# The first stage of a pool, retention and expert layer, cut into two phases without GpSimd's arithmetic, with the pool's window means moved among the gate products

## The chip, the cores and the metric

The kernel runs on one core of one Trainium2 chip. The metric is the device time of one execution in microseconds. TensorE does the matrix products, VectorE (DVE) and ScalarE (ACT) prepare their operands, GpSimd (POOL) helps with elementwise work and issues some transfers, and SyncE (SP) issues the loads of the weights.

## The reference, cut to what matters

512 tokens, width 2048, everything in fp32. What the change touches is the first half of the layer:

```python
mod = silu(c) @ w_ada + b_ada                       # 6 parts of 2048: sh1, sc1, g1, sh2, sc2, g2
hn = rmsnorm(x, norm_mix_gain) * (1 + sc1) + sh1
u_pool, q, k, v, g_ret, a_pool, a_ret = split(hn @ w_in)
pooled[g] = causal_window_mean(u_pool[g], w) - u_pool[g]     # g = 0..3, w = 2, 4, 8, 16
pool_out = (pooled[g] @ pool_w[g]) * pool_scale
q, k = rotary(q), rotary(k) / 16
y = retention(q, k, v)                              # 8 heads
merged = sigmoid(a_pool) * (pool_out @ w_branch_pool) + sigmoid(a_ret) * ((silu(g_ret) * layernorm(y)) @ w_branch_ret)
x = x + g1 * (merged @ w_out)
```

Then come the experts' queries, a selection among 16384 experts and two large products with their tables; the change does not touch them.

## The kernel before, in words

The activations stand transposed, as 16 tiles of 128 channels by 512 tokens. Each fp32 product is three matrix products of rounded operands (`mm3`, L85 to L87): a weight or activation is split into a high half (`whc`, `act`; ACT's cast at L73) and a low half (`wlc`, `act`; a subtraction at L74). A product of one block of 128 outputs (`gemm_t`) is 16 contraction steps, 48 matrix products; it takes its weights as two half chunks, and `half` converts the next half chunk while one is used. Weights arrive in chunks of 1 MB (`rawc`), loaded by SP's queue in the order of the list in `main_chunks`. There are three buffers each for `whc` and `wlc`.

`start` is the first stage. Its product for the first eight blocks of `u_pool` runs over the contraction outside and the blocks inside, since each channel's scale is found only then: for contraction step k, a chunk of `w_ada` is multiplied by silu(c) and summed on DVE (L188), the bias is added (L335), the scale is formed (L281), the input tile is scaled and split (L347 on ACT, L356 on DVE), and 24 matrix products run. `low_engine` puts the low halves of the weights on POOL here. POOL also adds up the squares (L205), and DVE fills in the rotary tables (L419 to L454). A second product over eight blocks follows in `pool_branch`, with the window sums (`window`, L513 and around) and four small products with `pool_w` (`mix`) between its blocks; then `shift` adds the shift of the modulation to all 16 tiles: POOL adds the halves (L397), DVE multiplies with 1/rms (L398), ACT and DVE split again (L403, L404). The retention needs the shifted tiles: its first product is q of head 0. After the eight heads come 32 gate products (`branches`, L670), whose results go to DRAM (`sig`), and then the products with the branch weights.

Inside `manual_schedule` the instructions of an engine stand as the code is written; elsewhere a scheduler orders them. Each engine works through its own queue in order.

Of the kernel before, what the change touches and what calls it, by code (L numbers as in the profile page):

```python
# [9 lines left out]
FT = mybir.dt.float32  # L10
# [19 lines left out]
POOL_JOBS = [('up', 0), ('up', 1), ('mix', 0), ('up', 2), ('up', 3), ('mix', 1), ('up', 4), ('up', 5), ('mix', 2), ('up', 6), ('up', 7), ('mix', 3)]  # L30
POOL_ADA = [1, 1, 1, 1, 2, 2, 2, 2, 2, 2, 0, 0]
# [16 lines left out]
class Mixer:  # L48
# [235 lines left out]
    def start(self):  # L284
        nc, a = self.nc, self.a
        stt = nc.vector.scalar_tensor_tensor
        self.cond_scope = ExitStack()
        cp = self.cond_scope.enter_context(self.tc.tile_pool(name="cp", bufs=1))
        with ExitStack() as cs:
            tp = lambda n, b=1: cs.enter_context(self.tc.tile_pool(name=n, bufs=b))  # L290
            p1, tmp, ap = tp("st1"), tp("st2", 3), tp("st3", 3)
            with self.tc.manual_schedule():
# [9 lines left out]
                seq = [(*self.ada(KT), ap), (a["w_up0"][0], None)]  # L302
                for k in range(1, KT):
# [4 lines left out]
                self.stream(seq + self.main_chunks())  # L308
                load(1)
                self.total = cp.tile([P, T], FT, name="total")  # L310
                banks = [self.bank() for _ in range(8)]
                self.hn = []
                raws = []
                table = self.rotary_tables(tmp)
                next(table)

                def low_half():
                    t, i = raws.pop(0)
                    h = self.wh.tile([P, D // 2], FR, name="whc")
                    l = self.wl.tile([P, D // 2], FR, name="wlc")  # L320
                    self.split(t[:, i * 1024:(i + 1) * 1024], h, l, nc.gpsimd)
                    self.ready.append((h, l))
# [6 lines left out]
                squares = 0  # L329

                def scale_in():
                    k = len(scaled)
                    self.consume()
                    m = slice(KT + k, KT + k + 1)
                    nc.vector.tensor_tensor(out=self.mod[:, m], in0=self.mod[:, m], in1=self.bada[:, m], op=OP.add)  # L335
                    self.scale_of(1, 0, 0, k)
                    scaled.append(self.sc[:, 0, k:k + 1])
                scaled = []
                scale_in()
                weights()  # L340
                low_half()
                for k in range(KT):
                    if k == 12:
                        self.ahead = 3
# [3 lines left out]
                    if k == 0:  # L348
                        stt(out=l, in0=xk[k], scalar=scaled[k], in1=h.bitcast(FT), op0=OP.mult, op1=OP.subtract)
                    if k + 1 < KT:  # L350
                        scale_in()
                        if k % 2:
                            weights()
                        low_half()
                    if k:
                        stt(out=l, in0=xk[k], scalar=scaled[k], in1=h.bitcast(FT), op0=OP.mult, op1=OP.subtract)  # L356
                    self.hn.append((h, l))
                    wh, wl = self.ready.pop(0)
# [5 lines left out]
                    if k >= 4:  # L364
                        for _ in (0, 1):
                            if squares < KT:
                                self.square(self.total, xk[squares], squares == 0, tmp, nc.gpsimd)
                                squares += 1
                    if k >= 2:
                        next(table, None)  # L370
                        next(table, None)
                for _ in table:
                    pass
                self.warm_sqrt(self.ones[:, 0:1])
                self.low_engine = nc.gpsimd
                self.convert()
                for i in (0, 1):
                    u = self.ring.tile([P, T], FT, name="act")
                    nc.scalar.copy(out=u, in_=banks[i])
                    banks[i] = u  # L380
                dg = self.diagonals(self.token_rms([self.total], cp), cp)
                self.r = cp.tile([P, T], FT, name="r")
                self.after(1, lambda: nc.scalar.copy(out=self.r, in_=self.spread(dg)))
                banks.append(self.gemm_t(self.hn))
            self.first_banks = banks

    def shift(self, pool):

        nc = self.nc
        m = slice(0, KT)
        nc.vector.tensor_tensor(out=self.mod[:, m], in0=self.mod[:, m], in1=self.bada[:, m], op=OP.add)
        for k, (h, l) in enumerate(self.hn):
            z = pool.tile([P, T], FT, name="hn")
            nc.gpsimd.tensor_tensor(out=z, in0=h.bitcast(FT), in1=l.bitcast(FT), op=OP.add)  # L397
            nc.vector.tensor_tensor(out=z, in0=z, in1=self.r, op=OP.mult)  # L398
            self.shifted(z, self.mod[:, k:k + 1], h, l)

    def shifted(self, z, sh, h, l):
        nc = self.nc
        nc.scalar.activation(out=h, in_=z, func=AF.Identity, bias=sh, scale=1.0)  # L403
        nc.vector.scalar_tensor_tensor(out=l, in0=z, scalar=sh, in1=h.bitcast(FT), op0=OP.add, op1=OP.subtract)  # L404

    def rotary_tables(self, tmp):
        nc, a = self.nc, self.a
        ts, stt = nc.vector.tensor_scalar, nc.vector.scalar_tensor_tensor
        self.cos = self.const.tile([P, T], FT, name="cos")
        self.sin = self.const.tile([P, T], FT, name="sin")  # L410
        invf = self.const.tile([P, 1], FT, name="invf")
        nc.gpsimd.dma_start(out=invf, in_=a["inv_freq"])
        pos = tmp.tile([P, T], I32, name="sq")
# [4 lines left out]
        r, h, n = self.sin, self.cos, tmp.tile([P, T], FT, name="rot", bufs=1)  # L418
# [37 lines left out]
    def main_chunks(self):  # L456
        a = self.a
        first = []
        for i, (what, n) in enumerate(POOL_JOBS):
            first.append((a["w_up1"][n] if what == "up" else a["pool_w"][GROUPS[n]], None))  # L460
            first += [self.ada(k) for k in range(sum(POOL_ADA[:i]), sum(POOL_ADA[:i + 1]))]
# [5 lines left out]
        seq += [a["w_ap"][i] for i in range(KT)] + [a["w_ar"][i] for i in range(KT)]  # L467
# [16 lines left out]
    def pool_branch(self):  # L484
# [3 lines left out]
        with ExitStack() as cs:  # L488
            tp = lambda n, b: cs.enter_context(self.tc.tile_pool(name=n, bufs=b))
            up, pk, ob, cp = tp("pu", 6), tp("pk", 8), tp("po", 3), tp("pc", 1)  # L490
            cnt = cp.tile([P, 4, PAD], FT, name="cnt")
            nc.gpsimd.dma_start(out=cnt, in_=a["inv_count"].to_broadcast([P, 4, PAD]))
            pooled = [[] for _ in GROUPS]

            def evacuate(bank):
                u = up.tile([P, PAD + T], FT, name="u")
                nc.vector.memset(u[:, :PAD], 0.0)
                nc.scalar.copy(out=u[:, PAD:], in_=bank)
                return u

            def window(turn, bank, raw=None):
                g = GROUPS[turn]
                u = evacuate(bank) if raw is None else up.tile([P, PAD + T], FT, name="u")
                if raw is not None:
                    nc.vector.memset(u[:, :PAD], 0.0)
                nc.vector.tensor_tensor(out=u[:, PAD:], in0=u[:, PAD:] if raw is None else raw, in1=self.r, op=OP.mult)
                s = u
                for lvl in range(g + 1):
                    w = 1 << lvl
                    s2 = up.tile([P, PAD + T], FT, name="u")  # L510
                    if lvl < g:
                        nc.vector.memset(s2[:, :PAD], 0.0)
                    nc.vector.tensor_tensor(out=s2[:, PAD:], in0=s[:, PAD:], in1=s[:, PAD - w:PAD + T - w], op=OP.add)  # L513
                    s = s2
                q = ob.tile([P, T], FT, name="pq")
                w = 2 << g
                nc.vector.tensor_tensor(out=q[:, :w], in0=s[:, PAD:PAD + w], in1=cnt[:, g, :w], op=OP.mult)
                nc.vector.tensor_tensor(out=q[:, :w], in0=q[:, :w], in1=u[:, PAD:PAD + w], op=OP.subtract)
                nc.vector.scalar_tensor_tensor(out=q[:, w:], in0=s[:, PAD + w:], scalar=1.0 / w, in1=u[:, PAD + w:],
                                               op0=OP.mult, op1=OP.subtract)  # L520
                h = pk.tile([P, T], FR, name="ph")
                l = pk.tile([P, T], FR, name="pl")
                self.split(q, h, l)
                pooled[turn].append((h, l))
# [19 lines left out]
            for what, i in POOL_JOBS:  # L544
                if what == "up":
                    window(2 + i // 4, self.gemm_t(self.hn) if i else self.first_banks[8])
                else:
                    if i == 3:
                        self.shift(ob)
# [766 lines left out]
```

## Time and profile before

| | |
|---|---|
| median of 3 runs | 4974.7 us (4973.16 to 4975.7) |
| profiled execution, its own time | 4985.34 us |
| its span | 4983.6 us |
| TensorE busy | 97% of the span |
| DVE, ACT, POOL busy | 65%, 34%, 32% |
| mean granted TensorE clock | 0.988 |

The profiled execution is 10.6 us longer than the median of the runs. A busy TensorE in these views includes the time in which matrix products overlap, so an idle TensorE is what to look for. The granted clock is given as a share of 2.4 GHz; it has two levels, 1.2 and 2.4 GHz.

### The profile page before, as it was taken

How to read it: one execution, taken by the hardware profiler on the slowest of the kernel's cores; microseconds unless marked ns; L12 is line 12 of the kernel's file. 1: busy time of each engine (PE TensorE's matmuls, PEld its weight loads, DVE VectorE, ACT ScalarE, POOL GpSimd, SP SyncE). 2: the span in 40 equal slices, each digit the busy share in tenths (PEclk: the TensorE clock that was granted, in tenths of full speed). 3: DMA queues.
4: the chain of work that ended last, by engine and by line, in shares of the span. 5: the costliest groups of instructions: out<-in, count | busy, mean ns of one | idle time of the engine just before them, and what ended most of it. 6: DMA issues, size and time to landing. Idle time of an engine off the chain costs nothing.

```text
span 4983.6 us, 58696 instructions
## 1 busy us (share of the span) xinstructions
PE 4832.4 (97%) x22905; PEld 4173.4 (84%) x22905; DVE 3237.4 (65%) x4296; ACT 1704.9 (34%) x2703; POOL 1570.5 (32%) x1125
## 2 busy tenths in 40 slices
PE   6889999999999999999989999999999999999998
PEld 5668888888888888888878999999999888888887
DVE  8873334434332245655567998888787688888876
ACT  3332222222222222222232346556566433332233
POOL 6440000000000010000010367777788344444433
PEclk9999999999999999999999999999999999999999
DMA  6442222222233356765732577887888989898884
GB/s 265 178 148 87 102 102 99 95 102 95 92 126 131 125 190 227 263 228 204 237 107 99 172 275 282 291 295 275 308 294 314 327 310 326 317 332 323 316 284 152
DMA packets 268454, 1058.12 MB, mean 212 GB/s; under 512 B 22656, under 2 KB 73904, under 8 KB 173328
## 3 DMA queue, kind: packets, MB, share of 16 engines
q1 hardware_dynamic: 208960, 726.71, 42.2%
q0 software_dynamic: 54416, 325.48, 17.2%
q8 instruction: 181, 2.97, 0.2%
q10 hardware_dynamic: 4800, 2.16, 0.2%
q14 instruction: 97, 0.79, 0.0%
HBM read 973.53 MB, written 80.75 MB: 212 GB/s over the span
## 4 chain that ended last, share of the span: by engine, by line
PE 72%; DVE 11%; issue 8%; DMA 5%; POOL 2%; ACT 2%; SPq 0%; POOLq 0%; DVEq 0%; ACTq 0%
PE bank L87 24%; PE bank L85 24%; PE bank L86 24%; DVE wlc L74 2%; DVE urow L978 1%; DVE rawc L188 1%; DMA gd<-gsc 1%; DMA rawc<-in_w_ada_dram 1%; POOL ohx L918 1%; DVE u L513 1%; DMA x<-m 1%; ACT whc L73 1%; PE bank L907 1%; DVE gsc L898 0%; DVE eq L869 0%
## 5 line engine op out<-in xcount | busy, mean ns | idle before, releaser
L74 DVE TENSOR_TENSOR wlc<-rawc,whc 128x1024 fp32r<-128x1024 f32 x905 | 1158.3, 1286 | 993.5 <-ACT whc L73 992.9
L73 ACT CAST whc<-rawc 128x1024 fp32r<-128x1024 f32 x968 | 998.9, 1050 | 1995.4 <-PE bank L86 1093.8
L85 PE MATMUL bank<-act,whc 128*128 128x512 f32 x2816 | 1101.8, 391 | 27.8 <-ACT act L347 19.0
L86 PE MATMUL bank<-act,whc 128*128 128x512 f32 x2816 | 1102.8, 392 | 24.1 <-DVE act L356 20.2
L87 PE MATMUL bank<-act,wlc 128*128 128x512 f32 x2816 | 1102.1, 391 | 6.4 <-POOL wlc L74 3.6
L87 PE MATMUL bank<-fh,wlc 128*128 128x384 f32 (+1 forms) x2304 | 792.7, 344 | 15.6 <-DVE wlc L74 12.9
L85 PE MATMUL bank<-fh,whc 128*128 128x384 f32 (+1 forms) x2304 | 793.3, 344 | 4.8 <-ACT whc L73 2.8
L86 PE MATMUL bank<-fl,whc 128*128 128x384 f32 (+1 forms) x2304 | 791.1, 343 | 0.7 <-DVE fl L734 0.5
L86 PEld LDWEIGHTS bank<-act,whc 128*128 128x128 f32 x2816 | 531.8, 189 | 141.0 <-DVE act L356 24.8
L85 PEld LDWEIGHTS bank<-act,whc 128*128 128x128 f32 x2816 | 532.1, 189 | 138.8 <-ACT act L347 19.0
L87 PEld LDWEIGHTS bank<-act,wlc 128*128 128x128 f32 x2816 | 531.8, 189 | 120.3 <-POOL wlc L74 4.9
L918 POOL TENSOR_SCALAR ohx<-iota,tr,gh 128x128 fp32r<-128x128 f32 x384 | 586.9, 1535 | 75.1 <-PE bank L907 70.7
L85 PE MATMUL bank<-whc,ph 128*128 128x512 f32 x1536 | 602.7, 392 | 1.0 <-ACT ph L73 1.0
L87 PE MATMUL bank<-whc,pl 128*128 128x512 f32 x1536 | 600.5, 391 | 0.0
L86 PE MATMUL bank<-wlc,ph 128*128 128x512 f32 x1536 | 597.7, 389 | 1.6 <-DVE wlc L74 1.6
L87 PEld LDWEIGHTS bank<-fh,wlc 128*128 128x128 f32 x2304 | 436.0, 189 | 30.3 <-DVE wlc L74 16.1
L85 PEld LDWEIGHTS bank<-fh,whc 128*128 128x128 f32 x2304 | 436.5, 189 | 15.7 <-ACT whc L73 4.0
L86 PEld LDWEIGHTS bank<-fl,whc 128*128 128x128 f32 x2304 | 436.0, 189 | 11.3 <-DVE fl L734 2.0
L929 POOL DMA_INDIRECT vrow<-in_v_dram,eidx x128 | 273.7, 2138 | 488.4 <-DVE accg L1076 473.2
L188 DVE SCALAR_TENSOR_TENSOR rawc<-rawc,cond 128x2048 f32<-128x2048 f32 x96 | 241.8, 2520 | 198.7 <-DMA rawc<-in_w_ada_dram 198.7
L86 PEld LDWEIGHTS bank<-wlc,ph 128*128 128x128 f32 x1536 | 288.4, 188 | 65.0 <-DVE wlc L74 2.4
L87 PEld LDWEIGHTS bank<-whc,pl 128*128 128x128 f32 x1536 | 288.2, 188 | 64.8 <-DVE pl L74 0.3
(285 smaller groups left out, 5292.9 us busy)
## 6 DMA issues: line engine op xcount, KB each, us to landing
rawc<-in_ut_dram SPq DMA_DIRECT2D x128, 1024.0 KB, 5.7
rawc<-in_v_dram SPq DMA_DIRECT2D x128, 1024.0 KB, 7.5
rawc<-in_w_ada_dram SPq DMA_DIRECT2D x96, 1024.0 KB, 5.3
rawc<-in_w_v_dram SPq DMA_DIRECT2D x32, 1024.0 KB, 4.9
rawc<-in_w_g_dram SPq DMA_DIRECT2D x32, 1024.0 KB, 4.8
rawc<-in_w_br_dram SPq DMA_DIRECT2D x32, 1024.0 KB, 5.0
ga<-gao SPq DMA_DIRECT2D x64, 384.0 KB, 6.8
gd<-gsc SPq DMA_DIRECT2D x24, 1024.0 KB, 10.1
```

Source lines behind the costliest of these rows:

```text
L73: nc.scalar.copy(out=h, in_=src)
L74: (eng or nc.vector).tensor_tensor(out=l, in0=src, in1=h.bitcast(FT), op=OP.subtract)
L85: mm(out, w[0], x[0], start=start, stop=False)
L86: mm(out, w[0], x[1], start=False, stop=False)
L87: mm(out, w[1], x[0], start=False, stop=stop)
L188: nc.vector.scalar_tensor_tensor(out=t, in0=t, scalar=1.0, in1=self.cond, op0=OP.mult, op1=OP.mult, accum_out=self.mod[:, j:j + 1])
L513: nc.vector.tensor_tensor(out=s2[:, PAD:], in0=s[:, PAD:], in1=s[:, PAD - w:PAD + T - w], op=OP.add)
L907: nc.tensor.matmul(bank[:, u * 2 * P:(u + 1) * 2 * P], y, x.rearrange("p h i -> p (h i)"), start=True, stop=True)
L918: nc.gpsimd.tensor_scalar(out=x[:, 0, :], in0=self.iota, scalar1=tr[:, 0, s], scalar2=gh[:, s].bitcast(FT), op0=OP.is_equal, op1=OP.mult)
L929: self.nc.gpsimd.indirect_dma_start(out=t, out_offset=None, in_=src, in_offset=bass.IndirectOffsetOnAxis(ap=self.eidx[:, k:k + 1], axis=0))
L978: nc.vector.scalar_tensor_tensor(out=u, in0=u, scalar=1.0, in1=fnat, op0=OP.mult, op1=OP.mult, accum_out=act[:, i:i + 1])
```

## The change

`start` is written anew in two phases. In the first, the contraction-outside product for eight blocks, all low halves are made by DVE; the bias is folded into the forming of the scale (`one`, L334); the sums of squares and the tables are gone from it. In the second phase the other eight blocks follow as plain `gemm_t` products; between them DVE adds the squares and multiplies the inputs with 1/rms in place, and the block results go to DRAM (`u`, `rd`) by POOL's queue. Then `shift` makes the 16 shifted tiles from the inputs (ACT forms the tile, DVE rounds and subtracts), and the two products of q of head 0 run in `start`, contraction outside, as the shifted tiles come. The rotary tables are made at the start of `retention`. `pool_branch` now hands out `window` and `mix`, which `branches` calls between the 32 gate products; each window loads its sums from DRAM, and there DVE makes the low halves of `pool_w`.

```diff
-                    self.split(t[:, i * 1024:(i + 1) * 1024], h, l, nc.gpsimd)
...
+                def convert():
+                    t, i = raws.pop(0)
+                    pair = self.next_pair()
+                    self.split(t[:, i * 1024:(i + 1) * 1024], *pair)
+                    return pair
...
-                    nc.vector.tensor_tensor(out=self.mod[:, m], in0=self.mod[:, m], in1=self.bada[:, m], op=OP.add)
-                    self.scale_of(1, 0, 0, k)
...
+                    stt(out=o, in0=self.mod[:, KT + k:KT + k + 1], scalar=one[:, k:k + 1],
+                        in1=self.gains[:, 0, k:k + 1], op0=OP.add, op1=OP.mult)
...
+                self.after(7, lambda: found.append(self.token_rms([total], cp)))
+                self.after(8, lambda: found.append(self.diagonals(found[0], cp)))
+                self.after(9, spread)
+                for k in range(KT):
+                    self.after(10 + k // 3, lambda k=k: over_rms(k))
+                for n in range(8):
+                    b = self.gemm_t(self.hn)
+                    self.after(1, lambda b=b, n=n: evacuate(8 + n, b))
...
+                    nc.scalar.activation(out=z, in_=xk[k], func=AF.Identity, bias=self.mod[:, k:k + 1],
+                                         scale=self.sc[:, 0, k:k + 1])
+                    nc.vector.tensor_copy(out=h, in_=z)
+                    tt(out=l, in0=z, in1=h.bitcast(FT), op=OP.subtract)
...
+                for kk in range(8):
+                    step(0, 0, kk, a0)
+                    step(1, 0, kk, b0)
+                b1 = convert()
+                for kk in range(4):
+                    step(0, 1, kk, a1)
+                for kk in range(4):
+                    step(0, 1, 4 + kk, a1)
+                    step(1, 1, kk, b1)
...
-        self.low_engine = None
-        self.cond_scope.close()
...
+            for _ in self.rotary_tables(tmp):
+                pass
...
+            window, mix = self.pool_branch(cs)
+            work = [(t, i) for t in range(4) for i in range(4)]
+            for j in range(2 * KT):
+                if work and j % 6 < 4:
+                    window(*work.pop(0))
+                b = self.gemm_t(self.hn) if j else self.first_gate
...
+                if j in MIXES:
+                    mix(MIXES.index(j))
```

In DVE's queue, one contraction step of the first product stood like this (`rawc` is a chunk of `w_ada`, `act` the low half of a scaled input tile, `sin` and `cos` the tables):

```order
L188 SCALAR_TENSOR_TENSOR rawc,mod<-rawc,cond 128x2048
L335 TENSOR_TENSOR mod<-mod,bada 128x1
L281 SCALAR_TENSOR_TENSOR sc<-mod,gains 128x1
L356 SCALAR_TENSOR_TENSOR act<-x_108,sc,act 128x512
L423 TENSOR_SCALAR cos<-sin 128x512
L425 TENSOR_SCALAR cos<-cos 128x512
```

Now DVE's queue begins so, `wlc` being the low half of a half chunk of weights:

```order
L306 TENSOR_SCALAR one<-bada 128x16
L188 SCALAR_TENSOR_TENSOR rawc,mod<-rawc,cond 128x2048
L334 SCALAR_TENSOR_TENSOR sc<-mod,one,gains 128x1
L74 TENSOR_TENSOR wlc<-rawc,whc 128x1024
L342 SCALAR_TENSOR_TENSOR act<-x_110,sc,act 128x512
L188 SCALAR_TENSOR_TENSOR rawc,mod<-rawc,cond 128x2048
```

The low half of the weights has come to DVE, and the bias and the tables have left the step.

At the handover to the retention DVE's queue was this in the kernel before (the last windows, `pq`, `pl`, and the shifted tiles, `hn`, `act`, side by side):

```order
L404 SCALAR_TENSOR_TENSOR act<-hn,mod,act 128x512
L517 TENSOR_TENSOR pq<-u,cnt 128x2
L519 SCALAR_TENSOR_TENSOR pq<-u 128x510
L518 TENSOR_TENSOR pq<-pq,u 128x2
L404 SCALAR_TENSOR_TENSOR act<-hn,mod,act 128x512
L398 TENSOR_TENSOR hn<-hn,r 128x512
L74 TENSOR_TENSOR pl<-pq,ph 128x512
```

Now it is this, for the last three shifted tiles (`rp_1614` is a scratch tile of the tables; `act` of L406 and L407 are the two halves of a shifted tile):

```order
L406 CAST act<-rawc 128x512
L463 TENSOR_SCALAR cos<-cos 128x512
L407 TENSOR_TENSOR act<-rawc,act 128x512
L406 CAST act<-rawc 128x512
L465 SCALAR_TENSOR_TENSOR sin<-cos,sin 128x512
L407 TENSOR_TENSOR act<-rawc,act 128x512
L406 CAST act<-rawc 128x512
L467 SCALAR_TENSOR_TENSOR rp_1614<-cos,sin 128x512
L407 TENSOR_TENSOR act<-rawc,act 128x512
L74 TENSOR_TENSOR wlc<-rawc,whc 128x1024 x2
```

The windows are gone from there; six instructions of the tables, from L457 on, stand among the last six shifted tiles, and the low half of the last half chunk of q's weights stands behind all of them.

Among the gate products DVE's queue held nothing but 60 low halves in a row. Now a stretch between two of them reads so (`raw` is a block's sums, loaded from DRAM; `pq` the mean less the value):

```order
L74 TENSOR_TENSOR wlc<-rawc,whc 128x1024
L74 TENSOR_TENSOR pl<-pq,ph 128x512
L552 TENSOR_TENSOR u<-u 128x512
L544 MEMSET u 128x16
L545 TENSOR_TENSOR u<-raw,r 128x512
L556 TENSOR_TENSOR pq<-u,cnt 128x4
L558 SCALAR_TENSOR_TENSOR pq<-u 128x508
L557 TENSOR_TENSOR pq<-pq,u 128x4
L74 TENSOR_TENSOR wlc<-rawc,whc 128x1024
```

And POOL's queue, where the loads of `raw` stand between the stores of the gates, begins there with:

```order
L542 DMA raw<-u 128x512 x2
L674 DMA ret<-ro 128x512 x4
L533 DMA cnt<-in_inv_count_dram 128x64
L535 DMA r<-rd 128x512
L705 DMA sig<-sg 128x512
L542 DMA raw<-u 128x512 x3
L705 DMA sig<-sg 128x512
L542 DMA raw<-u 128x512 x2
```

The window work is spread between the low halves instead of standing ahead of one of them, and five loads are issued ahead of the second gate's store.

## Rows read from the trace of the kernel before

**Rows 1.** The page: TensorE's busy tenths in 40 slices of the span.

```profile
PE   6889999999999999999989999999999999999998
```

**Rows 2.** Stages: window, length; each engine's busy us (instructions); clock, DMA share, GB/s.

```profile
0.00:19.00 19.00, 0.03 (x1) 0.03 (x1) 2.83 (x6) 4.94 (x5) 4.71 (x13) 1.00 0.89 327
19.00:140.00 121.00, 99.26 (x384) 77.33 (x385) 108.68 (x100) 38.80 (x54) 85.81 (x36) 0.94 0.60 230
140.00:327.40 187.40, 147.93 (x593) 116.18 (x592) 172.70 (x228) 60.59 (x86) 97.83 (x50) 0.89 0.49 174
327.40:349.20 21.80, 21.80 (x97) 18.05 (x97) 11.19 (x12) 6.40 (x8) 4.05 (x6) 1.00 0.55 196
371.10:414.40 43.30, 43.30 (x193) 35.85 (x192) 15.81 (x18) 11.31 (x13) 0.00 (x0) 1.00 0.28 93
1480.00:1820.00 340.00, 340.00 (x1510) 281.76 (x1509) 85.29 (x76) 90.74 (x106) 24.89 (x47) 1.00 0.39 137
```

**Rows 3.** TensorE's waits from 19 to 330 us: total, times, longest.

```profile
PE bank L85 <- ACT ph L73: 23.2, 4, 14.3
PE bank L86 <- DVE act L356: 20.2, 11, 3.0
...
PE bank L86 <- DVE pl L74: 7.5, 3, 4.4
```

**Rows 4.** Timeline of DVE, POOL, ACT at the start: start us, duration us.

```profile
14.86 2.29 DVE L188 SCALAR_TENSOR_TENSOR rawc<-rawc,cond 128x2048 f32<-128x2048 f32 x1 [13.86 <-DMA rawc<-in_w_ada_dram]
...
17.25 1.04 ACT L73 CAST whc<-rawc 128x1024 fp32r<-128x1024 f32 x1 [9.40 <-DMA rawc<-in_w_up_dram]
...
18.38 5.13 POOL L74 TENSOR_TENSOR wlc<-rawc,whc 128x1024 fp32r<-128x1024 f32 x2 [13.28 <-ACT whc L73]
...
18.96 2.33 DVE L349 SCALAR_TENSOR_TENSOR act<-x,sc,act 128x512 fp32r<-128x512 f32 x1 [1.41 <-ACT act L347]
...
21.21 4.45 DVE L188 SCALAR_TENSOR_TENSOR rawc<-rawc,cond 128x2048 f32<-128x2048 f32 x1
```

**Rows 5.** Groups by shape on DVE and POOL, up to 350 us: total, mean ns.

```profile
L335 DVE TENSOR_TENSOR mod<-mod,bada 128x1 f32<-128x1 f32 x16 | 20.6, 1286 | 0.6
...
L425 DVE TENSOR_SCALAR cos<-cos 128x512 f32<-128x512 f32 x1 | 0.4, 427 | 0.0
...
L394 DVE TENSOR_TENSOR mod<-mod,bada 128x16 f32<-128x16 f32 x1 | 0.2, 175 | 0.0
...
L74 POOL TENSOR_TENSOR wlc<-rawc,whc 128x1024 fp32r<-128x1024 f32 x41 | 120.0, 2932 | 106.5 <-ACT whc L73 106.5
```

**Rows 6.** Groups by shape on DVE, 400 to 1400 us, and on ACT, to 350 us.

```profile
L74 DVE TENSOR_TENSOR wlc<-rawc,whc 128x1024 fp32r<-128x1024 f32 x168 | 205.5, 1223 | 446.7 <-ACT whc L73 446.7
...
L74 DVE TENSOR_TENSOR vl<-bank,vh 128x512 fp32r<-128x512 f32 x28 | 19.3, 690 | 12.3 <-ACT vh L73 12.3
...
L403 ACT ACTIVATE act<-hn,mod 128x512 fp32r<-128x512 f32 x16 | 11.5, 723 | 16.8 <-DVE hn L398 14.6 <-PE bank L87 2.0
```

**Rows 7.** Timeline of TensorE: after a wait, and the first and last start of q.

```profile
84.50 0.79 PE L86 MATMUL bank<-act,whc 128*128 128x512 f32 x1 [2.95 <-DVE act L356]
85.09 0.63 PE L87 MATMUL bank<-act,wlc 128*128 128x512 f32 x1
85.52 0.63 PE L85 MATMUL bank<-act,whc 128*128 128x512 f32 x1
...
327.47 0.40 PE L85 MATMUL bank<-act,whc 128*128 128x512 f32 x1
...
349.24 0.39 PE L85 MATMUL bank<-act,whc 128*128 128x512 f32 x1
```

**Rows 8.** DMA, to 350 us: GB/s in 40 slices; issues, count, KB, us to landing.

```profile
GB/s 235 402 424 419 408 288 270 167 193 167 195 167 315 120 25 100 114 143 224 163 110 290 275 124 152 209 197 297 241 184 285 220 259 120 120 1 2 187 232 110
...
mixed<-pm POOLq DMA_DIRECT2D x16, 256.0 KB, 6.5
...
sq<-in_positions_dram POOLq DMA_DIRECT2D x1, 256.0 KB, 9.9
```

More of the change, by code (lines that the diff above doesn't have):

```diff
@@ L301, in start @@
                 load(0)
-                seq = [(*self.ada(KT), ap), (a["w_up0"][0], None)]
-                for k in range(1, KT):
+                one = cp.tile([P, KT], FT, name="one")
+                nc.vector.tensor_scalar(out=one, in0=self.bada[:, KT:2 * KT], scalar1=1.0, scalar2=None, op0=OP.add)
+                seq = []
+                for k in range(KT):
                     seq.append((*self.ada(KT + k), ap))
@@ L385, in start @@
[L385 to L404, printed above, removed]
+                def evacuate(i, bank):
+                    u = tmp.tile([P, T], FT, name="u")
+                    nc.scalar.copy(out=u, in_=bank)
+                    nc.gpsimd.dma_start(out=self.u[i], in_=u)
+                total = cp.tile([P, T], FT, name="total")
@@ new lines, in start, with spread, over_rms @@
+                r = cp.tile([P, T], FT, name="r")
+                found = []
+                def spread():
+                    nc.scalar.copy(out=r, in_=self.spread(found[1]))
+                    nc.gpsimd.dma_start(out=self.rd, in_=r)
+                def over_rms(k):
+                    tt(out=xk[k], in0=xk[k], in1=r, op=OP.mult)
+                evacuate(0, banks[0])
+                evacuate(1, banks[1])
+                for i in range(2, 8):
+                    self.after(i // 2, lambda i=i: evacuate(i, banks[i]))
@@ new lines, in start @@
+                a0 = self.ready.pop(0)
+                t0 = self.loaded.pop(0)[0]
+                t1 = self.loaded.pop(0)[0]
+                raws[:] = [(t1, 0), (t0, 1), (t1, 1)]
+                shift(0)
+                shift(1)
+                self.tick()
+                b0 = convert()
+                shift(2)
+                shift(3)
+                a1 = convert()
+                for k in range(4, KT):
+                    shift(k)
+                self.fill()
+                out = [self.bank(), self.bank()]
@@ L406, in rotary_tables @@
+                self.convert()
+                for kk in range(4, 8):
+                    step(1, 1, kk, b1)
+                self.flush()
+                self.first_q = out
+        self.ahead = 3
     def rotary_tables(self, tmp):
@@ L551, in pool_branch @@
-        self.low_engine = None
-        self.cond_scope.close()
+        tp = lambda n, b: cs.enter_context(self.tc.tile_pool(name=n, bufs=b))
+        up, pk, ob, cp = tp("pu", 4), tp("pk", 8), tp("po", 2), tp("pc", 1)
+        cnt = cp.tile([P, 4, PAD], FT, name="cnt")
+        nc.gpsimd.dma_start(out=cnt, in_=a["inv_count"].to_broadcast([P, 4, PAD]))
+        r = cp.tile([P, T], FT, name="r")
+        nc.gpsimd.dma_start(out=r, in_=self.rd)
+        pooled = [[] for _ in GROUPS]
+        tt = nc.vector.tensor_tensor
@@ new lines, in mix @@
+        def mix(turn):
+            banks = [self.bank() for _ in range(4)]
+            for hf in (0, 1):
+                h, l = self.half()
+                for n in range(4):
+                    for kk in (0, 1):
+                        k = 2 * hf + kk
+                        s = slice(kk * T + n * P, kk * T + (n + 1) * P)
+                        self.mm3(banks[n], (h[:, s], l[:, s]), pooled[turn][k], k == 0, k == 3)
+            for n in range(4):
+                o = ob.tile([P, T], FT, name="pm")
+                j = 4 * GROUPS[turn] + n
+                nc.scalar.mul(out=o, in_=banks[n], mul=self.gains[:, 1, j:j + 1])
+                nc.gpsimd.dma_start(out=self.mixed[j], in_=o)
```

222 lines of the change are left out of this document (90 added, 132 removed).

## Prediction

> **What bounds the kernel now.** I read the page's slices first: TensorE is busy everywhere except at the left edge, so an edit pays only there or where it adds products [rows 1]. The table by stages shows how wide the edge is. From 19 to 140 us 384 products run, from 140 to 327.4 us the other 576 up to the first of q, and TensorE is idle for 21.7 and 39.5 us of these stretches; the granted clock is 0.94 and 0.89 of 2.4 GHz, so part of the rest ran at 1.2 GHz [rows 2]. At full clock the 96 products of q start 21.77 us apart, 0.227 each [rows 7]. 960 products would be 218 us; the stage takes 327.5. Everything from 349.2 us on (k of head 0 and later) keeps its order, so the change is read off two things: when q ends, 349.2 us now, and what the gate products take.
>
> Next the waits. TensorE waits 20.2 us for DVE's low half of the inputs (11 times, in the first product), 23.2 us for the pooled operands on ACT, once 14.3 us (at the fourth small product), and 7.5 us for their low halves [rows 3]. DVE is the late one, 172.7 busy of 187.4 us [rows 2]. Why it is late shows in the timeline: the chunk of `w_ada` takes 2.29 us at 14.86, with POOL idle, and 4.45 us at 21.21, and a 512-wide low half 2.33 us at 18.96, both beside POOL's low half, which begins at 18.38 [rows 4]. Even the one-column bias add means 1.29 us, where a 16-column one alone took 0.175, and POOL needs 2.93 us for a low half [rows 5] that DVE makes in 1.22 once POOL is quiet [rows 6]. So the two hold each other up.
>
> **First product.** DVE's step becomes: chunk 2.29 [rows 4], scale 0.18 (by the 16-column add, [rows 5]), low half of the weights 1.22, low half of the input 0.69 [rows 6]; 4.4 us. TensorE's step is 24 x 0.227 = 5.44, so TensorE sets the pace and nothing on DVE shows. The loads: a step takes 1.5 MB of chunks and, until the inputs are in, another 0.25 MB; 1.8 MB in 5.44 us is 340 GB/s, and the queue has moved 402 to 424 [rows 8]. The start itself: weights cast at 17.25 + 1.04 [rows 4], low half 1.22, input 0.69: the second product can start at 20.2 us. The first step's 23 further products end at 30.1 at the half clock (0.43 apart, [rows 7]) and at 25.4 at the full one; I take 27.8. Then 15 x 5.44 = 81.6: **109.4 us**, where it was 140.
>
> **Second phase.** 384 products, 87.1 us. DVE has 16 chunks (36.6), 16 low halves (19.5), 31 adds and multiplications of 512 (21.4) and some 2 of small ones: 80 of 87. That fits, but in order, and one place does not: DVE waits for the sums of 1/rms, which TensorE forms in the middle of the fourth block; behind that wait stand seven small instructions (1.2), two chunks (4.6) and the next low half (1.2), 7.0 us against the 5.44 of the half block that TensorE still has. A wait of 2 us with the semaphores. The 16 small products for 1/rms: between nothing (they stand in the old stage too, and no row prices one here) and 16 x 0.227 = 3.6; I take 1.6. **200 us.** The block results go out by POOL's queue beside it, and nothing waits for them here.
>
> **Handover to q.** From the end of the eighth block, t = 0. Two shifted tiles are ready. q's second block needs its first half chunk: ACT copies a block out (0.72 as an ACT pass of 512, [rows 6]), casts (1.04), DVE subtracts (1.22): t = 3.0, and TensorE has 0.7 us of work. Wait 2.3. DVE then makes a tile in 0.43 + 0.69 = 1.12 (the rounding copy is not in the trace; between the 0.43 of a one-operand pass [rows 5] and 0.69, and I take the first since it has one operand too), against TensorE's 6 x 0.227 = 1.36, so steps 0 to 7 run through to t = 13.2. DVE's queue: two tiles and a low half to 6.5, tiles 4 to 9 to 13.2, tiles 10 to 15 with six instructions of the tables (4 x 0.43 + 2 x 0.69) to 23.0, the last low half to 24.2. TensorE runs out after step 12 of the first block, t = 18.5, and waits 5.7; then 11 x 0.68 = 7.5 remain: 31.7. After a wait of 3 us the rows show a stretch at 0.43 apart [rows 7]; 2 us for that. **q ends at 234 us**, 115 earlier.
>
> One load stands in this chain: the first table instruction (L457) needs the positions, which POOL loads after the last block's store. The store took 6.5 us to land, the positions 9.9, both beside other transfers [rows 8]; with ACT's copy they would be there at t = 17, and L457 is due at 14.3: up to 3 us more. With an idle queue it is nothing; I take nothing.
>
> The Trainium skill (SBUF — State Buffer, "SBUF: two separate sides") says that a transfer issued by GpSimd needs its descriptors written by GpSimd, which is locked out of the port while DVE runs an fp32 copy in its two-port mode, and gives 620 ns grown to 3100. That speaks against the 16 rounding copies beside these two issues; by it the positions come some 5 us later and the sum is 4911. No row here has such a copy beside such an issue.
>
> **Gate products.** The 192 small products move here: 43.5 us, since TensorE is busy throughout: 340 of 340 us [rows 2]. The window work on DVE: 16 windows with 88 passes of 512, 0.69 each, 61 us; DVE was busy 85 of 340 us there. Between two low halves, 5.44 us apart, the order has about seven passes and the low half, 6.0 us at the most crowded place, and with three buffers a low half may be made up to two halves early. Cost 0 while that lead lasts. Behind the fourth small product ACT waits for the branch's first loads, which need the memory of the windows: 6.5 us to land against a lead of 5.4 to 10.9; I take 3 for all of this. The tables' other 16 instructions stand at the retention's start, some 10 us of DVE spread over k and v, where DVE is busy 15.8 of 43.3 us [rows 2] and the scores need q only 65 us later: nothing. If this cover were gone, it would cost their 10 us.
>
> **Sum.** -115.2 + 43.5 + 3 = -68.7 us. The profiled execution took 4985.3: 4916.6. It lies 10.6 above the median of the runs: **4906 us**.
>
> **Bounds.** Best: first step 25.4, no wait anywhere, q over at 216: 4885. Worst: first step 30.1 (+2.3), DVE a tenth late in the second phase (+8), positions late (+3), rounding copy at 0.69 (+4), gates +10: 4933.
>
> **The rivals.**
> - *Transfers bound the new start.* Until k's weights some 57 chunks and 17 stores, 64 MB, must move. At 340 GB/s it is 190 us, hidden; at the 288 of the slice after the first rush [rows 8] it is 223, and with the handover q ends 20 us later: 4926. For it: eight blocks ask for 24 chunks and 4 MB of stores in 87 us. Against: 402 to 424 in four slices.
> - *DVE stays slow without POOL*, because the transfers slow it. Its step would stay near 6 us, 10 us more in the first product and 17 in the second phase: 4933. Against: 2.29 us at 14.86, while the DMA share was 0.89 and POOL idle. The skill's same section holds that transfers and engines have separate ports; the trace agrees.
> - *Slower than before: the windows stall the gates.* If DVE's queue held a window ahead of the next low half and its load stood behind the last gate's store, each window would cost: sigmoid 0.7, landing 6.5, window 3.8, low half 1.2, less the 5.4 of lead, 6.8 us; 16 times 109: 4906 + 109 = 5015. It decides at 4.3 us a window (68.7 / 16), a landing of 4.0. Against: in the order the loads stand two or more gates ahead of their use and the passes are spread.
> - *A milder form*: each window costs 2.5 us, by waits of DVE for ACT inside it: 4946.
>
> **How the numbers follow.** Forecast 0.73, transfers 0.10, slow DVE 0.06, mild gates 0.07, slow gates 0.04. The range 4885 to 4936 takes in the forecast's bounds and the first two rivals. A measurement of this kernel tells a change of about 0.2%, 10 us, from none: faster 0.95, same 0.01, slower 0.04.
>
> **What would show it.** The first 384 products over by about 109 us with chunks of 2.3 us on DVE; the eight blocks over by 200; two waits of TensorE in q, of about 2 and 6 us, the second for a `wlc` behind the tables; q over by 234; the gate stage 43 to 47 us longer, with DVE some 60 us busier. The prediction is wrong if the clock falls repeatedly in the first 200 us, if TensorE waits for `rawc` there, or if it waits for `wlc` among the gates.

## The result and the profile after

The changed kernel takes 4900.9 us (median of 4 runs, 4894.5 to 4907.4) against 4975.2 (4 runs, 4973.2 to 4981.4): ratio 0.9849, 95% interval 0.9832 to 0.9866, 74 us less. Its profiled execution took 4907.44 us, with a span of 4905.7.

The page's row of TensorE's busy tenths in 40 slices, which answers to [rows 1]:

```profile
PE   8999999999999999999999999999999999999998
```

The left edge is filled; of its first slice only the 17.1 us up to the first product are lost. The stages (as in [rows 2]: window, length, busy us and instructions of PE, PEld, DVE, ACT, POOL, clock, DMA share, GB/s) are first product, eight blocks, q, and the gates:

```profile
17.10:108.20 91.10, 90.60 (x384) 74.39 (x385) 68.18 (x79) 29.29 (x36) 1.46 (x3) 1.00 0.84 339
108.20:202.70 94.50, 91.42 (x401) 74.77 (x400) 76.47 (x93) 33.57 (x49) 7.19 (x14) 0.98 0.74 284
202.70:233.60 30.90, 25.05 (x97) 19.21 (x96) 28.37 (x50) 15.32 (x20) 2.16 (x4) 0.89 0.30 102
1364.50:1758.00 393.50, 391.65 (x1736) 324.01 (x1735) 159.86 (x251) 125.08 (x157) 48.59 (x90) 1.00 0.46 160
```

The first product has 0.5 us without TensorE where the 121 us of before had 21.7, DVE works 68 of 91 us, and the granted clock is given as 1.00; the products up to 24.5 us start 0.43 us apart all the same, and only those behind them 0.23. What TensorE waited for up to 420 us, which answers to [rows 3]:

```profile
PE bank L85 <- ACT act L341: 17.1, 1, 17.1
PE bank L87 <- DVE wlc L74: 7.9, 4, 4.3
PE bank L85 <- ACT whc L73: 1.0, 1, 1.0
PE bank L86 <- DVE act L342: 0.5, 1, 0.5
```

The 17.1 are the start. The 20.2 us for `act` have become 0.5, and the 30.7 for pooled operands (23.2 and 7.5) are gone. Four waits for low halves of weights, made by DVE, stand where the kernel before had four for those made by GpSimd (19 to 330 us):

```profile
PE bank L87 <- POOL wlc L74: 5.5, 4, 1.9
```

DVE's groups by shape in the first product (total, mean ns | idle before):

```profile
L188 DVE SCALAR_TENSOR_TENSOR rawc<-rawc,cond 128x2048 f32<-128x2048 f32 x15 | 34.3, 2286 | 1.2 <-DMA rawc<-in_w_ada_dram 1.2
L74 DVE TENSOR_TENSOR wlc<-rawc,whc 128x1024 fp32r<-128x1024 f32 x18 | 22.0, 1224 | 21.1 <-ACT whc L73 21.1
L342 DVE SCALAR_TENSOR_TENSOR act<-x,sc,act 128x512 fp32r<-128x512 f32 x16 | 11.9, 746 | 0.0
L334 DVE SCALAR_TENSOR_TENSOR sc<-mod,one,gains 128x1 f32<-128x1 f32 x15 | 3.3, 219 | 0.5
```

The chunk and the low half of the weights have the durations that they had before where POOL was quiet [rows 4 and 6]; the low half of the input and the scale take 0.75 and 0.22 us, where the prediction took 0.69 and 0.18 from the nearest rows. DVE idles 21 us for ACT's cast, so TensorE sets the pace and not DVE.

The four waits for low halves come two and two. DVE's timeline in the second block, and then TensorE's behind the wait at the start of the third (start, duration; the idle time before in brackets):

```profile
124.99 2.28 DVE L188 SCALAR_TENSOR_TENSOR rawc<-rawc,cond 128x2048 f32<-128x2048 f32 x1
...
131.62 1.22 DVE L74 TENSOR_TENSOR wlc<-rawc,whc 128x1024 fp32r<-128x1024 f32 x1
...
132.90 0.50 PE L87 MATMUL bank<-act,wlc 128*128 128x512 f32 x1 [2.03 <-DVE wlc L74]
```

Three chunks of `w_ada` in a row (6.6 us) stand between the square sums and the low half that TensorE needs at 130.9. At the start of the fifth block, behind the small instructions for 1/rms and two chunks:

```profile
158.55 0.50 PE L87 MATMUL bank<-act,wlc 128*128 128x512 f32 x1 [1.05 <-DVE wlc L74]
```

At the handover to q:

```profile
204.53 0.50 PE L85 MATMUL bank<-act,whc 128*128 128x512 f32 x1 [0.98 <-ACT whc L73]
...
205.79 0.50 PE L87 MATMUL bank<-act,wlc 128*128 128x512 f32 x1 [0.53 <-DVE wlc L74]
...
224.80 0.79 PE L87 MATMUL bank<-act,wlc 128*128 128x512 f32 x1 [4.29 <-DVE wlc L74]
```

### The profile page after: what moved, and what is told of

It is laid out like the page before. It is cut to its first block, busy times and chain, and to the rows that moved or that the text cites. A ratio compares the mean times of both kernels' runs of the same rounds, so it can differ in the third digit from the quotient of the medians.

```text
span 4905.7 us, 58734 instructions
## 1 busy us (share of the span) xinstructions
PE 4814.1 (98%) x22905; PEld 4166.2 (85%) x22905; DVE 3185.0 (65%) x4353; ACT 1706.5 (35%) x2704; POOL 1442.4 (29%) x1087
## 4 chain that ended last, share of the span: by engine, by line
PE 72%; issue 10%; DVE 9%; DMA 5%; ACT 2%; POOL 2%; SPq 0%; DVEq 0%; POOLq 0%; ACTq 0%
PE bank L87 24%; PE bank L85 23%; PE bank L86 23%; DVE wlc L74 2%; DVE urow L1016 2%; DMA gd<-gsc 2%; DMA rawc<-in_w_ada_dram 2%; POOL ohx L956 1%; ACT whc L73 1%; DVE gsc L936 1%; DMA x<-m 1%; PE bank L945 0%; DVE rawc L188 0%; DVE eq L907 0%; DVE ohx L958 0%
## 5 line engine op out<-in xcount | busy, mean ns | idle before, releaser
L74 DVE TENSOR_TENSOR wlc<-rawc,whc 128x1024 fp32r<-128x1024 f32 x946 | 1203.2, 1278 | 992.4 <-ACT whc L73 991.5
L85 PE MATMUL bank<-act,whc 128*128 128x512 f32 x2816 | 1101.2, 391 | 21.7 <-ACT act L341 17.1
L87 PE MATMUL bank<-act,wlc 128*128 128x512 f32 x2816 | 1101.0, 391 | 11.3 <-DVE wlc L74 11.3
L85 PEld LDWEIGHTS bank<-act,whc 128*128 128x128 f32 x2816 | 531.4, 189 | 133.3 <-ACT act L341 17.1
L87 PEld LDWEIGHTS bank<-act,wlc 128*128 128x128 f32 x2816 | 531.4, 189 | 124.7 <-DVE wlc L74 14.6
L956 POOL TENSOR_SCALAR ohx<-iota,tr,gh 128x128 fp32r<-128x128 f32 x384 | 616.8, 1614 | 55.7 <-PE bank L945 51.5
L86 PEld LDWEIGHTS bank<-fl,whc 128*128 128x128 f32 x2304 | 436.2, 189 | 10.9 <-DVE fl L772 1.7
L85 PEld LDWEIGHTS bank<-whc,ph 128*128 128x128 f32 x1536 | 288.4, 188 | 60.8 <-ACT ph L73 1.3
```

The lines of the kernel that those rows point to most:

```text
L74: (eng or nc.vector).tensor_tensor(out=l, in0=src, in1=h.bitcast(FT), op=OP.subtract)
L85: mm(out, w[0], x[0], start=start, stop=False)
L86: mm(out, w[0], x[1], start=False, stop=False)
L87: mm(out, w[1], x[0], start=False, stop=stop)
L956: nc.gpsimd.tensor_scalar(out=x[:, 0, :], in0=self.iota, scalar1=tr[:, 0, s], scalar2=gh[:, s].bitcast(FT), op0=OP.is_equal, op1=OP.mult)
```

## The experiments

Landmarks of every trace, in us from the span's start. Each is the start of a product on TensorE, "first product over" that of the product behind it; the last column is from the first branch product to the last product of the kernel:

| kernel | first product over | first of q | first of k | first branch product | from there |
|---|---|---|---|---|---|
| before | 140.0 | 327.5 | 349.2 | 1827.7 | 3138.1 |
| after | 108.2 | 202.7 | 233.6 | 1757.8 | 3130.7 |
| e1_pool_scratch | 130.2 | 224.6 | 255.0 | 1778.4 | 3127.6 |
| e2_before_low_dve | 128.2 | 315.7 | 337.5 | 1816.4 | 3120.9 |
| e3_before_no_pool | 122.8 | 289.3 | 311.1 | 1789.5 | 3133.1 |
| e4_gates_late | 107.2 | 201.5 | 231.9 | 1846.6 | 3132.1 |
| e5_pool_scratch_small | 122.4 | 215.6 | 246.1 | 1769.1 | 3128.8 |
| e6_squares_early | 107.8 | 196.6 | 226.8 | 1749.4 | 3131.7 |
| e7_handover | 106.9 | 200.1 | 223.8 | 1745.7 | 3126.3 |
| e8_both | 108.4 | 197.3 | 220.9 | 1742.8 | 3126.9 |
| e9_both_timed | 107.2 | 196.1 | 219.7 | 1741.9 | 3128.7 |
| e10_after_timed | 107.2 | 201.4 | 231.8 | 1753.8 | 3126.8 |

The last column is one and the same code in all twelve and spreads over 17 us; before's profiled execution is the longest of them. So edits are read off the four columns ahead of it. The runs e1 to e8 are single executions. The changed kernel stands in the table twice (after, e10): its first product, eight blocks and q differ by 1.0, 0.3 and 0.5 us, its first branch product by 4.0.

**GpSimd work that nobody waits for (e1_pool_scratch).** Theory: GpSimd and DVE hold each other up. Rivals: DVE was late because it waited for GpSimd's results, or because of the loads.

```diff
+                idle = tmp.tile([P, 2 * T], FT, name="idle", bufs=1)
                 def scale(k):
+                    nc.gpsimd.tensor_tensor(out=idle, in0=self.cond[:, :2 * T], in1=self.cond[:, 2 * T:], op=OP.subtract)
```

> The changed kernel with 16 subtractions of 128x1024 on GpSimd, all in a row from about 10 us on, into a scratch tile that nothing reads; no other instruction waits for them. Theory (GpSimd and DVE hold each other up while both work): the 16 take about 5 us each, so until some 90 us; while they run DVE's step is the 8.4 us of the kernel before instead of 4.4 (chunk 4 to 4.5 us, low half of the weights about 2.4), TensorE's step follows it, and the first 384 products are over at 125 to 140 us instead of 108.2, with the rest unchanged: 4901 + 25. Rival 1 (DVE was late because it waited for GpSimd's results): nothing waits here, so 108 plus or minus 2, chunks 2.3. Rival 2 (the loads slow DVE): the loads are the same, 108 too.

One step of DVE's timeline, and GpSimd's scratch instructions, the first alone and 15 beside DVE:

```profile
42.44 4.45 DVE L188 SCALAR_TENSOR_TENSOR rawc<-rawc,cond 128x2048 f32<-128x2048 f32 x1
...
46.93 2.23 DVE L334 SCALAR_TENSOR_TENSOR sc<-mod,one,gains 128x1 f32<-128x1 f32 x1
49.09 1.21 DVE L74 TENSOR_TENSOR wlc<-rawc,whc 128x1024 fp32r<-128x1024 f32 x1
50.23 2.83 DVE L345 SCALAR_TENSOR_TENSOR act<-x,sc,act 128x512 fp32r<-128x512 f32 x1
...
7.87 2.34 POOL L341 TENSOR_TENSOR idle<-cond 128x1024 f32<-128x1024 f32 x1 [3.82 <-ACT cond L303]
...
10.73 52.31 POOL L341 TENSOR_TENSOR idle<-cond 128x1024 f32<-128x1024 f32 x15
```

The 4.45 of [rows 4] is back to the hundredth, with no result of GpSimd in the chain and with the same loads, which moved more slowly than in the changed kernel (a DMA share of 0.63 while GpSimd works): both rivals are out. But three instructions of very different size are lengthened by the same 2.0 to 2.2 us (2.29 to 4.45, 0.22 to 2.23, 0.75 to 2.83), a little less than one GpSimd instruction. DVE's step is 10.5 us, not the 8.4 expected, and lasts until GpSimd ends at 63 instead of 90; 130.2 us for the first product is in the range by two errors that cancel. Total 4924.9.

**The same elements in shorter instructions (e5_pool_scratch_small).** If the two take turns by whole instructions, halving GpSimd's halves what each DVE instruction pays. The edit, against the run before:

```diff
-                    nc.gpsimd.tensor_tensor(out=idle, in0=self.cond[:, :2 * T], ...
+                    for _ in (0, 1):
+                        nc.gpsimd.tensor_tensor(out=idle, in0=self.cond[:, :T], in1=self.cond[:, T:2 * T], op=OP.subtract)
```

> As the run with scratch subtractions on GpSimd, but 32 of 128x512 instead of 16 of 128x1024: the same elements in instructions half as long (1.17 us alone, by half of 2.34). Theory (the two take turns by whole instructions: each of the three scalar_tensor_tensor of DVE's step waits for the end of the GpSimd instruction under way, whatever its own size): the three are lengthened by about 1.0 us each instead of 2.0 to 2.2, so the chunk takes 3.3, the one-column scale 1.2, the low half of the input 1.8, DVE's step 7.6 us instead of 10.55, while GpSimd lasts to 80 to 100 us instead of 63; first product over at 122 to 130. Rival (they share the port's rate, so the same elements cost the same): chunk 4.4, one-column scale 2.2, step 10.5 us until about 63.

The step of DVE in this run, and GpSimd's instructions:

```profile
49.77 3.37 DVE L188 SCALAR_TENSOR_TENSOR rawc<-rawc,cond 128x2048 f32<-128x2048 f32 x1
...
53.19 1.12 DVE L334 SCALAR_TENSOR_TENSOR sc<-mod,one,gains 128x1 f32<-128x1 f32 x1
54.23 1.21 DVE L74 TENSOR_TENSOR wlc<-rawc,whc 128x1024 fp32r<-128x1024 f32 x1
55.37 1.76 DVE L346 SCALAR_TENSOR_TENSOR act<-x,sc,act 128x512 fp32r<-128x512 f32 x1
...
7.63 1.26 POOL L342 TENSOR_TENSOR idle<-cond 128x512 f32<-128x512 f32 x1 [3.58 <-ACT cond L303]
...
9.41 70.68 POOL L342 TENSOR_TENSOR idle<-cond 128x512 f32<-128x512 f32 x31
```

Lengthened by 1.1, 0.9 and 1.0: turns it is. GpSimd's 31 take 2.28 us each instead of 1.26, and DVE's step 7.28. The Trainium skill (SBUF — State Buffer, "Who interferes with whom") says that a DVE instruction with two inputs in SBUF and a GpSimd instruction that reads SBUF exclude each other for a whole instruction; the two traces agree, with these numbers. The low half between them (1.21 us) pays nothing in either trace although it has two such inputs. GpSimd pays there: in e1 its next instruction begins 0.14 us behind the low half (49.09) and takes 3.29 us instead of 2.34, in e5 it begins 0.14 behind (54.37 and 54.23) and takes 2.20 instead of 1.26.

```profile
49.23 3.29 POOL L341 TENSOR_TENSOR idle<-cond 128x1024 f32<-128x1024 f32 x1
```

**Only the low halves of the first product off GpSimd, in the kernel before (e2_before_low_dve).**

```diff
-                    self.split(t[:, i * 1024:(i + 1) * 1024], h, l, nc.gpsimd)
+                    self.split(t[:, i * 1024:(i + 1) * 1024], h, l)
```

> The kernel before with one edit: the low halves of the weights of the first product are made by DVE instead of GpSimd; GpSimd keeps the squares there and all its work behind. Theory: DVE's step without GpSimd beside it is chunk 2.29, bias 0.18, scale 0.18, low halves 1.22 and 0.69, two table instructions 1.1, 5.7 us against the 5.44 of TensorE; where GpSimd adds two squares a step (8 steps) DVE loses 1 to 2 us more. First product over at 113 to 127 instead of 140, all behind it shifted by as much: total 13 to 27 less than 4975. Rival (the new order, not GpSimd, brings it): 140, no change.

The first product is over at 128.2, just beyond the range, and the branch products begin 11.3 us earlier, just short of it; the rival, no change, is out. The total, 4955.6 against 4981.0 beside it, flatters the edit: its last column is the shortest of all. GpSimd's 15 remaining squares still cost: the chunk means 2575 ns.

**All of GpSimd's arithmetic off, the old order kept (e3_before_no_pool).** Theory: this is the smaller part of the gain. Rival: it is the whole gain.

```diff
-                    self.split(t[:, i * 1024:(i + 1) * 1024], h, l, nc.gpsimd)
+                    self.split(t[:, i * 1024:(i + 1) * 1024], h, l)
...
-                                self.square(self.total, xk[squares], squares == 0, tmp, nc.gpsimd)
+                                self.square(self.total, xk[squares], squares == 0, tmp)
...
-                self.low_engine = nc.gpsimd
...
-            nc.gpsimd.tensor_tensor(out=z, in0=h.bitcast(FT), in1=l.bitcast(FT), op=OP.add)
+            nc.vector.tensor_tensor(out=z, in0=h.bitcast(FT), in1=l.bitcast(FT), op=OP.add)
```

> The kernel before with all arithmetic of GpSimd in the first stage given to DVE (low halves, squares, the sums of the halves in the shift); its order is kept. Theory: in the first product DVE has 5.7 us a step, 7.1 where two squares are added: over at 118 to 124. From there to q, DVE gets the sums and the low halves of the pool products and the blocks (about 41 us) and loses the slowing down (about as much): some 172 us of DVE for a stretch of 187, so that stage stays at 180 to 190 and q ends at 320 to 335 instead of 349: total about 20 less than 4975, against 74 less for the whole change. So most of the change would come from what was moved away from this stage. Rival (taking GpSimd out is the whole gain): the stage falls to 145 to 155, q ends at 285 to 295, total 4915 to 4920.

DVE's groups in the first product:

```profile
L188 DVE SCALAR_TENSOR_TENSOR rawc<-rawc,cond 128x2048 f32<-128x2048 f32 x15 | 34.3, 2285 | 1.4 <-DMA rawc<-in_w_ada_dram 1.4
...
L335 DVE TENSOR_TENSOR mod<-mod,bada 128x1 f32<-128x1 f32 x15 | 2.4, 160 | 0.5
```

The stage from there to q, by window:

```profile
122.60:288.80 166.20, 141.09 (x592) 113.72 (x591) 151.29 (x271) 62.78 (x87) 7.32 (x14) 0.92 0.55 198
```

TensorE's waits from 122 to 311 us:

```profile
PE bank L87 <- DVE wlc L74: 24.8, 4, 13.9
```

The one-column add goes from 1286 ns [rows 5] to 160, the first product ends at 122.8 as expected, but the stage behind it takes 166.5 us (expected 180 to 190, the rival 145 to 155): I had counted 172 us of undisturbed DVE work, and it is 151.3. At the first branch product the edit is worth 38.2 of the whole change's 69.9 us. So some 38 come with GpSimd's arithmetic off and some 32 with the new order on top of it. Of these 32, 14.6 lie in the first product (over at 108.2 against 122.8), which no longer holds the squares, the tables and the bias; the rest lies behind it, where the windows no longer share DVE with the stage: here TensorE still waits 24.8 us for DVE. What each move of the new order is worth by itself was not tried. Neither expectation had this. Total 4941.8.

**The gates without a lead (e4_gates_late).** The order is written by hand, and each mix has its four windows directly ahead of it.

```diff
-                if work and j % 6 < 4:
-                    window(*work.pop(0))
+            with self.tc.manual_schedule():
...
                     if j in MIXES:
+                        for _ in range(4):
+                            window(*work.pop(0))
                         mix(MIXES.index(j))
```

> The changed kernel with the gate products and their windows in an order written by hand: the four windows of a mix stand directly ahead of its small products, on every queue. Theory (the window work is free only because it is made some gates ahead): before each mix TensorE waits for the first load (0.7 sigmoid, 6.5 landing), four windows of about 5.4 us with their split and the low half, less the 5.4 of the first half of the mix: about 24 us, four times, and a stretch at half clock behind each: the gate stage 95 to 110 us longer than in the changed kernel, total about 5000, slower than before. Rival (DVE is so idle there that the place does not matter): 0 to 10 us longer.

The gate stage by window:

```profile
1364.50:1846.50 482.00, 416.36 (x1720) 333.94 (x1719) 161.84 (x250) 121.38 (x154) 50.24 (x93) 0.92 0.37 132
```

TensorE's waits in it:

```profile
PE bank L85 <- ACT ph L73: 49.0, 8, 10.0
PE bank L85 <- ACT whc L73: 14.9, 5, 5.5
```

The first window of the first mix in DVE's timeline:

```profile
1431.36 0.69 DVE L545 TENSOR_TENSOR u<-raw,r 128x512 f32<-128x512 f32 x1 [11.40 <-DMA raw<-u]
```

482.0 us against 393.5, with 2 us more of DVE work: 88.5 longer, under the 95 to 110 expected. The waits are smaller (17 us a mix, not 24) and what follows them dearer: TensorE's busy time grows by 24.7 us, the clock falling from 1.00 to 0.92. Total 4997.8, 17 more than the kernel before beside it. So the slower rival named a real mechanism: 88.5 / 16 = 5.5 us a window, beyond its turning point of 4.3. In the changed kernel, where the windows have a lead, the stage has one wait of 1.9 us. The edit does two things, though: it takes the lead away and it fixes every queue of the stage by hand. No run fixed the order with the lead kept, so how the 88.5 divide between the two is not shown. The line above, DVE waiting 11.4 us for a load with no lead, is of the first kind.

**Squares in the first product (e6_squares_early)**, **two conversions earlier at the handover (e7_handover)**, and **both (e8_both)**, to see whether the four new waits are the places of single instructions.

In e6 1/rms is formed at half blocks 2 to 4 instead of 7 to 9, the multiplications with it follow from the fifth half block on, and a square stands in each step of the first product from the third on:

```diff
+                        if k >= 2:
+                            self.square(total, xk[k - 2], k == 2, tmp)
...
-                    self.after(1 + k // 3, lambda k=k: self.square(total, xk[k], k == 0, tmp))
```

In e7 the first conversion goes ahead of the copy of the eighth block, the second behind the twelfth shifted tile:

```diff
-                self.tick()
                 b0 = convert()
+                self.tick()
...
-                for k in range(4, KT):
+                for k in range(4, 12):
                     shift(k)
...
                 b1 = convert()
+                for k in range(12, KT):
+                    shift(k)
```

> The changed kernel with the squares and their sum moved from the first blocks of the second phase into the first product, one a step, and 1/rms two blocks earlier. Theory (DVE has slack in the first product, 68 of 91 us busy, and none in the second and third block, where it had 13.4 us of work in 10.9): first product over at 108 to 109 as now, TensorE's waits of 2.2 and 1.2 us in the second phase gone, the eight blocks over at 198.5 to 200 instead of 202.7, q as long as now (30.9): 3 us less in all. Rival (the added pass makes DVE late in the first product): first product over at 112 or later, no gain.

> The changed kernel with two conversions moved at the handover: the second block's first half chunk ahead of the copy of the eighth block, and its second half chunk behind the twelfth shifted tile instead of behind the sixteenth and the tables. Theory (TensorE's waits there come from the place of these low halves in DVE's and ACT's queues, and the half clock from the waits): waits of 1.5 and 4.3 us become 0 and 0 to 1.5, 2 us less at half clock; q takes 24.5 to 27 us instead of 30.9 and is over at 227 to 230. Rival (DVE is short in sum, 16 tiles of 1.1 and four low halves being 22.6 us for 21.8 of TensorE): the wait only moves to the tiles, q takes 29 to 31.

> Both of these edits together. Theory: the eight blocks over at 198.5 to 200, q over at 223 to 227 instead of 233.6, total 7 to 10 us less than the changed kernel. Rival (as DVE is freed, the loads or ACT become late): q over at 230 or later.

TensorE's waits in e6, 19 to 240 us:

```profile
PE bank L87 <- DVE wlc L74: 4.8, 2, 4.3
PE bank L85 <- ACT whc L73: 1.0, 1, 1.0
```

The same in e7:

```profile
PE bank L87 <- DVE wlc L74: 2.9, 2, 1.9
PE bank L85 <- DVE act L406: 0.7, 1, 0.7
```

In e8, to 420 us:

```profile
PE bank L85 <- ACT act L341: 17.4, 1, 17.4
PE bank L85 <- DVE act L409: 0.7, 1, 0.7
PE bank L86 <- DVE act L342: 0.5, 1, 0.5
```

Its first product, eight blocks and q, by window:

```profile
17.30:108.40 91.10, 90.52 (x384) 74.33 (x385) 78.39 (x95) 38.19 (x53) 1.46 (x3) 1.00 0.85 339
108.40:197.20 88.80, 88.80 (x401) 73.86 (x400) 66.74 (x79) 25.99 (x34) 7.18 (x14) 1.00 0.79 302
197.20:220.90 23.70, 22.76 (x98) 17.87 (x98) 21.73 (x40) 14.49 (x19) 2.15 (x4) 1.00 0.44 133
```

Each edit takes away its own two waits and leaves the other pair. e6: eight blocks in 88.8 us instead of 94.5, more than the 3 to 4 expected, since besides 3.1 us of waits the products 0.43 apart behind the first of them went. e7: q in 23.7 us instead of 30.9, again better than expected; its rival, DVE short in sum, is out. e8 has both, with q over at 220.9 where 223 to 227 were expected, and the first product unchanged with 78 us of DVE in 91.

Last, both edits and the changed kernel itself, timed side by side.

> The kernel with both edits again, timed against the kernel before. In the traces it gained 15 us on the changed kernel up to the branch products (1742.6 against 1757.5), and that part repeats to within some 2 us, while the experts' stage moves by up to 9 us either way from one run to the next. So its median should lie 13 to 17 us below that of the changed kernel timed beside it, at 4884 to 4892, a ratio to before of 0.981 to 0.984. Rival (the gain is one run's luck): within 5 us of the changed kernel.

> The changed kernel itself, unedited, timed beside the run above: 4901 plus or minus 4, ratio 0.985.

Over 5 rounds on one chip, both edits: 4889.6 us (4888.1 to 4891.9), ratio to before 0.9822 (0.9809 to 0.9836); the changed kernel: 4899.4 (4891.3 to 4901.0), 0.9836 (0.9822 to 0.9851). The medians lie 9.8 us apart, between the 13 to 17 expected and the rival's 5. The expectation had been taken from the first trace of the changed kernel; beside this one the first branch product comes 11.9 us earlier. The times hardly overlap, the intervals do: the gain is shown by the traces, its size in the total only roughly.

## Why the prediction was right, and where it was off

- **What bounds.** Right: the time came out of the left edge and went into the gates. At the first branch product the gain is 69.9 us; the sum was 68.7. That it comes so near is partly luck: the steps below were off by 1.2 early, 3.9 late, 2.8 early and 0.8 early, and the first branch product of the same kernel in e10 comes 4.0 us earlier again.
- **The mechanism.** "The two hold each other up" is shown by e1 and e5, with a sharper form: by turns, one whole instruction each. The rival that DVE stays slow is out: 2286 ns a chunk at a DMA share of 0.84. e3 adds that taking GpSimd's arithmetic away alone gives some 38 of the 70 us.
- **First product,** 109.4: measured 108.2. From the 25th product at 26.6 it runs 15 x 5.44 = 81.6 us, as worked out. The start, a middle between two bounds, was taken 1.2 us too late.
- **Second phase,** 90.6 us: measured 94.5, the one step that failed in kind. The wait behind 1/rms came (1.0, predicted 2), and the small products cost 1.7 (88.8 - 87.1 in e8; taken as 1.6). But "80 of 87" was a balance over the whole phase: in the second block DVE had three chunks, six square sums and two low halves, 13.4 us of work in 10.9, and TensorE waited 2.0 us behind it, with its products 0.43 apart for a while after. e6 shows it: with the sums spread out both are gone.
- **Handover,** 33.7: measured 30.9. The two places were right and both too dear: 1.5 instead of 2.3, 4.3 instead of 5.7. A rounding copy takes 0.42 us, as taken, but DVE's instructions start closer together than they last: the last six tiles with their table instructions took 8.2 us (215.30 to 223.53), summed up as 9.8. The positions were issued at 206.95, in 0.54 us as elsewhere, and L457 ran at 215.63 without a wait. The delay of 5 us that the prediction estimated by the Trainium skill (SBUF — State Buffer, "SBUF: two separate sides") did not show at this one issue, which a rounding copy overlapped for 0.2 us.
- **Transfers** were no bound: 339 and 284 GB/s. Up to 234 us ACT's casts waited 7.6 us for weights of `u_pool`, 2.1 at most, and DVE 1.2 us for chunks; no wait of TensorE stands behind these.
- **Gates,** 46.5 us: from the first of k to the first branch product 1478.5 became 1524.2, 45.7 more (43.5 in e10), with one wait of 1.9 us for the first branch operands. In e4, without the lead and with the queues fixed by hand, the stage is longer by 88.5 us, more than the whole gain.
- **The total.** 4906 against a median of 4900.9. The sum's error makes 1.2 of these 5 us; the medians themselves are known to some 8 (the interval of the ratio). The profiled execution gained 7.4 us more behind the first branch product, in code that is the same; that column spreads over 17 us, and why it does was not tried and stays open.

## What to carry to other kernels

GpSimd's elementwise work beside a busy DVE cost DVE here about one GpSimd instruction for each of its own that had to wait its turn, however short; compare an instruction's duration with the other engine quiet and busy before giving GpSimd "idle" time. Balance an engine's queue block by block and not over a stage, and look for the instruction that stands ahead of a needed operand: moving 15 sums (with 1/rms behind them) and two conversions took 12 us out of a stage whose sums already fitted. Work moved under a saturated TensorE needs a lead: the same windows cost some 2 us in all a few gates ahead, and 5.5 us each directly ahead of their use in an order fixed by hand.

## What was not expected of the hardware

- The turns themselves: a one-column instruction of 0.22 us took 2.23 beside 2.34 us instructions of GpSimd and 1.12 beside 1.26 us ones; GpSimd's own went to 3.5 and 2.3.
- How far waits reach by the clock, and that they do not always: in q, waits of 1.0, 0.5 and 4.3 us went with a mean granted clock of 0.89 and 30.9 us (0.94 and 30.4 us in e10, the same kernel); with none over 0.7 the clock was 1.00 and q took 23.7, 7.2 less for 5.8 of waits. In the gates of e4, 68 us of waits went with 25 us more of busy time. At the start of the third block the wait of 2.0 us was followed by a stretch at 0.43 apart, while one of 1.9 us at the same place in e7 was not, and the eight blocks there kept a clock of 1.00.
